# Two of thirteen norm factors: an integer guess and Newton steps on VectorE in the place of ScalarE's square root

## The chip, the cores and the metric

The kernel runs on one core of a Trainium2 chip. The metric is the device time of one execution in microseconds (us), the median of the runs shown; lower is better. The engines are TensorE (PE for its matmuls, PEld for its weight loads), VectorE (DVE), ScalarE (ACT), GpSimd (POOL) and SyncE (SP, which issues the DMAs). Each engine works through its own instructions in order; semaphores order them between engines.

## What is computed

A network of two layers on 1024 tokens of width 1024, in float32. Layer 0 mixes by sliding-window attention, layer 1 by a gated recurrence; each is followed by an MLP with a squared ReLU. Every block begins with a norm over the token's 1024 numbers:

```python
def rmsnorm(x, gain):
    y = x * lax.rsqrt(jnp.mean(jnp.square(x), axis=-1, keepdims=True) + NORM_EPS)
    return y * gain

for layer in range(2):
    h = rmsnorm(x, mix_norm[layer])
    y = attention(h, ...) if layer == 0 else recurrence(h, ...)
    x = x + y
    x = x + square(relu(rmsnorm(x, mlp_norm[layer]) @ w_up)) @ w_down
return rmsnorm(x, final_norm)
```

The factor of a token is one number, `rsqrt(mean(x*x) + eps)`. In attention the norm is taken before the projection to queries, keys and values, and the factor is applied to the projection's result, since it is the same for a whole token.

## The kernel before

The tokens are handled in two halves of 512 (`hf` 0 and 1). A matrix product in float32 is made of three fast products of parts (`mm3`: high by high, high by low, low by high), so a 512-wide weight block costs a cast to the high part (`wh`), a subtraction for the low part (`wl`) and three matmuls for each result bank.

All work is first recorded and then put in order by a planner (`Schedule.order`): it has a modelled cost for every operation and a modelled latency from engine to engine, and gives each engine, whenever it would be free, the ready operation that was recorded earliest (with leads for weights and for emptying banks). So the order in which the engines work is fixed when the program is built, and every operation that is added, removed or costed otherwise can move others. All instructions are issued from one line (L334), so the rows of the profile tell operations apart by engine, kind and the tag of the tiles: `a` long-lived 128x512 tiles, `t` short-lived ones, `m` scores and masks, `sm` tiles of 128x4, `wr`/`wh`/`wl` weights as loaded and their high and low parts, `c` constants, `p` and `q` the banks of PSUM (four each).

What the change and the argument touch:

- `token_rstd` (line 450) makes the factors of one half's tokens: four tiny matmuls (128x1 each) give the mean squares of 4 x 128 tokens in a `q` bank, a tensor_scalar adds eps (`v`, an `sm` tile), ScalarE takes a square root of 128x4 numbers, VectorE takes the reciprocal, and three VectorE operations make one Newton step (`y*y`, times `-0.5*v`, plus 1.5, times `y`).
- It is called in six places of the code. `scaled` (line 481) is one; it is used only in attention, once for each half (lines 1215 and 1219).
- `qkv` (line 1058) projects; `projected` applies the factor when it empties a `p` bank. `rope` rotates the keys and queries, and TensorE transposes them (`q<-c,t`, `q<-c,a`).
- `attend` (line 1115) transposes the queries of a group of heads, four blocks to a `q` bank (`q<-c,a`). Each bank is then read by two ScalarE instructions (`a<-q`, high parts) and two VectorE instructions (`a<-q,a`, low parts), one for each half of its rows; the bank is free for the next use when the second of the two VectorE instructions has read it.
- `attend_block` (line 1155) makes scores (`q<-a,a` and `q<-t,a`), masks them on VectorE into `m`, takes the maximum (`sm<-m`), the exponentials on ScalarE, the reciprocal of the sum and the product (`m<-m,sm`), and transposes the result (`q<-c,m`).
- Attention of half 0 is interleaved with the projection of half 1 (line 1220), so TensorE has projection matmuls (`p<-wh,a`, `p<-wl,a`) between the attention's steps.

A function on ScalarE that is not in its current table is preceded by an ACT_TABLE_LOAD, which the compiler puts in: Sqrt, Sin (the rotation tables), Exp and Tanh each bring one when the one before was another.

Of the kernel before, what the change touches and what calls it, by code (L numbers as in the profile page):

```python
# [12 lines left out]
I32 = mybir.dt.int32  # L13
AF = mybir.ActivationFunctionType
ALU = mybir.AluOpType
# [5 lines left out]
KT = D // P  # L21
NH = 2
TH = T // NH
# [256 lines left out]
class Net:  # L280
# [166 lines left out]
            acc = sq if acc is None else acc  # L447
        return acc

    def token_rstd(self, acc, inner=1.0, outer=1.0, n=TH, keep=False, more=()):  # L450

        ps = self.psum("q")
        nb = n // P
        for j in range(nb):
            parts = [acc, *more]
            for i, z in enumerate(parts):
                self.mm(ps[:, j : j + 1], z[:, j * P : j * P + P], self.mean, i == 0, i == len(parts) - 1, P, 2)
        v, y, z = (self.t(F32, (P, BPH), "sm")[:, :nb] for _ in range(3))
        self.ts("DVE", v, ps[:, :nb], inner, EPS, ALU.mult, ALU.add, 4)
        self.act(y, v, AF.Sqrt, 4)  # L460
        self.op("DVE", self.nc.vector.reciprocal, [y], [y], 100, y, y)
        self.tt("DVE", z, y, y, ALU.mult, 4)
        self.stt(z, v, -0.5 * outer, z, ALU.mult, ALU.mult, 4)
        if keep:
            y, r = self.const((P, BPH)), y
        else:
            r = y
        self.stt(y, z, 1.5 * outer, r, ALU.add, ALU.mult, 4)
        return y

    def spread(self, y, n=TH, r=None):

        r = (r or self.psum("q"))[:, :n]
        for j in range(n // P):
            self.mm(r[:, j * P : j * P + P], y[:, j : j + 1].to_broadcast([P, P]), self.ident, True, True, P, 4)
        return r
# [4 lines left out]
    def scaled(self, which, hf):  # L481

        h = []
        for kt in range(KT):
            x, gain = self.x[kt][hf], self.gain(which, kt)
            hi, lo = self.a(F32R), self.a(F32R)
            self.act(hi, x, AF.Copy, scale=gain)
            self.stt(lo, x, gain, hi.bitcast(F32), ALU.mult, ALU.subtract)
            h.append((hi, lo))
        return h, self.token_rstd(self.sum_squares([self.x[kt][hf] for kt in range(KT)]))  # L490


    def square_relu(self, m, hf, c, psum):
# [1151 lines left out]
```

## Time and profile before

| | us |
|---|---|
| median of 3 runs (2117.57 to 2119.33) | 2118.83 |
| the profiled execution, its own time | 2122.58 |
| its span on the core | 2120.8 |
| PE busy in the span | 2093.9 |
| DVE busy | 1902.4 |
| ACT busy | 1120.4 |
| DMA moved | 407 MB, 192 GB/s on the mean |

The profiled execution lies 3.75 us above the median and has 1.78 us outside the span. A busy share is an average over stages: attention (to about 300 us) is made of many short instructions on four engines, the rest of long rows of matmuls.

### The profile page before, as it was taken

The page shows a single profiled execution, that of the slowest core. Times are in us where ns is not written, and L with a number is a line of the kernel's source. Part 1 is how long each engine was busy: PE and PEld are TensorE (multiplying, and loading weights), DVE is VectorE, ACT ScalarE, POOL GpSimd, SP SyncE. Part 2 cuts the span into 40 slices and gives each one's busy share as a digit, 9 for nine tenths or more (in the row PEclk, how much of TensorE's full clock was granted, in tenths as well). Part 3 has the DMA queues.
Part 4 walks back from the last instruction along what each step waited for, and adds up shares of the span by engine and source line. Part 5 has one row for each costly group of instructions (what it writes and reads, how often), then busy time and mean ns, then how long its engine had stood idle before and what let it go on. Part 6 is the DMA issues. An engine that isn't in the chain of part 4 may idle for free.

```text
span 2120.8 us, 35631 instructions
## 1 busy us (share of the span) xinstructions
PE 2093.9 (99%) x12220; PEld 1741.4 (82%) x12220; DVE 1902.4 (90%) x3925; ACT 1120.4 (53%) x2280; POOL 60.3 (3%) x121
## 2 busy tenths in 40 slices
PE   9999999999999999999999999999999999999998
PEld 7778778888888888888888888888788888888887
DVE  8889899999999989999888888888999999898985
ACT  5567776655565323556444444452755656432453
POOL 4020000000000000000000000000000000000000
PEclk9999999999999999999999999999999999999999
DMA  6212268867778967632222222666876767896732
GB/s 205 84 52 74 87 215 272 283 224 244 230 243 285 313 222 253 221 134 75 100 95 95 100 96 87 205 231 218 272 268 227 245 227 251 283 319 217 246 108 80
DMA packets 225845, 407.43 MB, mean 192 GB/s; under 512 B 25344, under 2 KB 30464, under 8 KB 225664
## 3 DMA queue, kind: packets, MB, share of 16 engines
q1 hardware_dynamic: 225664, 405.16, 56.8%
q8 instruction: 96, 1.57, 0.3%
q14 instruction: 85, 0.70, 0.1%
HBM read 321.17 MB, written 83.89 MB: 191 GB/s over the span
## 4 chain that ended last, share of the span: by engine, by line
PE 87%; DVE 7%; issue 2%; ACT 2%; DMA 1%; POOL 0%; POOLq 0%; SPq 0%; ACTq 0%; DVEq 0%
PE p L334 46%; PE q L334 42%; DVE t L334 3%; DVE a L334 2%; DVE m L334 1%; ACT t L334 1%; ACT a L334 1%; DVE wl L334 1%; DMA a<-in_x 0%; DMA c<-in_par 0%; DVE wh L334 0%; DMA t<-d 0%; DVE sm L334 0%; DMA d<-a 0%; POOL a L334 0%
## 5 line engine op out<-in xcount | busy, mean ns | idle before, releaser
L334 PE MATMUL p<-a,wh 128*128 128x512 f32 (+1 forms) x2880 | 817.2, 367 | 0.2 <-ACT t L334 0.2
L334 PE MATMUL q<-a,wh 128*128 128x512 f32 x2112 | 662.6, 395 | 2.2 <-ACT t L334 1.7
L334 PEld LDWEIGHTS p<-a,wh 128*128 128x128 f32 x2880 | 514.3, 188 | 93.0 <-ACT t L334 0.7
L334 PE MATMUL p<-a,wl 128*128 128x512 f32 (+1 forms) x1440 | 524.1, 364 | 1.8 <-DVE wl L334 1.7
L334 PEld LDWEIGHTS q<-a,wh 128*128 128x128 f32 x2112 | 389.0, 188 | 87.1 <-ACT t L334 3.0
L334 PE MATMUL q<-a,wl 128*128 128x512 f32 x1056 | 416.0, 394 | 1.1 <-DVE wl L334 1.1
L334 PEld LDWEIGHTS p<-a,wl 128*128 128x128 f32 x1440 | 270.9, 188 | 47.0 <-DVE wl L334 3.0
L334 DVE TENSOR_TENSOR wl<-wr,wh 128x512 fp32r<-128x512 f32 x352 | 240.3, 684 | 6.4 <-ACT wh L334 1.4
L334 DVE TENSOR_TENSOR wl<-m,wh 128x512 fp32r<-128x512 f32 x338 | 230.2, 685 | 9.8 <-ACT wh L334 0.3
L334 PEld LDWEIGHTS q<-a,wl 128*128 128x128 f32 x1056 | 198.3, 188 | 47.9 <-DVE wl L334 1.5
L334 ACT ACTIVATE t<-t 128x512 f32<-128x512 f32 x266 | 167.6, 632 | 124.3 <-DVE t L334 118.3
L334 ACT CAST wh<-wr 128x512 fp32r<-128x512 f32 x247 | 152.6, 619 | 151.7 <-PE p L334 104.6
L334 DVE TENSOR_TENSOR t<-t,t 128x512 f32<-128x512 f32 (+3 forms) x337 | 196.8, 598 | 16.7 <-DMA t<-d 10.3
L334 ACT CAST a<-t 128x512 fp32r<-128x512 f32 (+1 forms) x213 | 128.3, 611 | 148.2 <-PE q L334 83.1
L334 DVE TENSOR_TENSOR a<-t,a 128x512 fp32r<-128x512 f32 (+2 forms) x314 | 205.5, 675 | 1.1 <-ACT a L334 0.8
L334 ACT CAST wh<-m 128x512 fp32r<-128x512 f32 x231 | 143.3, 621 | 111.5 <-PE p L334 48.7
L334 ACT COPY t<-q 128x512 f32<-128x512 f32 (+2 forms) x201 | 112.4, 560 | 104.6 <-PE q L334 91.4
L334 DVE TENSOR_TENSOR m<-wr,wr 128x512 f32<-128x512 f32 (+1 forms) x188 | 120.9, 645 | 15.6 <-DMA wr<-in_down 12.9
L334 PE MATMUL p<-wh,a 128*128 128x512 f32 x384 | 127.9, 404 | 2.3 <-ACT a L334 2.3
L334 DVE TENSOR_TENSOR t<-t,p 128x256 f32<-128x256 f32 x294 | 117.4, 412 | 0.2
L334 PEld LDWEIGHTS q<-t,t 128*64 128x64 f32 (+1 forms) x2160 | 95.4, 144 | 13.9 <-issue 7.8
L334 PE MATMUL q<-t,t 128*64 128x32 f32 (+2 forms) x2160 | 105.4, 229 | 0.0
(129 smaller groups left out, 2396.3 us busy)
## 6 DMA issues: line engine op xcount, KB each, us to landing
t<-d SPq DMA_DIRECT2D x548, 256.0 KB, 4.0
d<-t SPq DMA_DIRECT2D x244, 256.0 KB, 2.7
wr<-in_down SPq DMA_DIRECT2D x224, 256.0 KB, 4.2
wr<-in_up SPq DMA_DIRECT2D x178, 256.0 KB, 3.8
wr<-in_win SPq DMA_DIRECT2D x68, 256.0 KB, 2.6
a<-d SPq DMA_DIRECT2D x60, 256.0 KB, 4.5
wr<-in_wqkv SPq DMA_DIRECT2D x48, 256.0 KB, 2.7
d<-a SPq DMA_DIRECT2D x48, 256.0 KB, 3.7
```

The lines of the kernel that those rows point to most:

```text
L334: fn(*[place(a) for a in args], **{k: place(v) for k, v in kw.items()})
```

## The change

`scaled` asks for factors without the table. For these two calls the square root on ScalarE and the reciprocal on VectorE fall away. In their place stand two integer operations (shift the bits of `v` right by one, and subtract from a constant), which give a first guess of `1/sqrt(v)`, and two Newton steps more, of three operations each; the third step is the one that was there. The other eleven executions of `token_rstd` keep the square root.

```diff
-    def token_rstd(self, acc, inner=1.0, outer=1.0, n=TH, keep=False, more=()):
+    def token_rstd(self, acc, inner=1.0, outer=1.0, n=TH, keep=False, more=(), table=True):
...
         self.ts("DVE", v, ps[:, :nb], inner, EPS, ALU.mult, ALU.add, 4)
-        self.act(y, v, AF.Sqrt, 4)
-        self.op("DVE", self.nc.vector.reciprocal, [y], [y], 100, y, y)
+        if table:
+            self.act(y, v, AF.Sqrt, 4)
+            self.op("DVE", self.nc.vector.reciprocal, [y], [y], 100, y, y)
+        else:
+            self.guess(y, v)
+            for _ in range(2):
+                self.tt("DVE", z, y, y, ALU.mult, 4)
+                self.stt(z, v, -0.5, z, ALU.mult, ALU.mult, 4)
+                self.stt(y, z, 1.5, y, ALU.add, ALU.mult, 4)
         self.tt("DVE", z, y, y, ALU.mult, 4)
...
+    def guess(self, y, v):
+
+        bits = y.bitcast(I32)
+        self.ts("DVE", bits, v.bitcast(I32), 1, None, ALU.logical_shift_right, None, 4)
+        self.ts("DVE", bits, bits, -1.0, float(0x5F3759DF), ALU.mult, ALU.add, 4)
...
-        return h, self.token_rstd(self.sum_squares([self.x[kt][hf] for kt in range(KT)]))
+        return h, self.token_rstd(self.sum_squares([self.x[kt][hf] for kt in range(KT)]), table=False)
```

ScalarE has four instructions fewer (two square roots and two of eight table loads), VectorE fourteen more. Apart from the numbers in the tiles' names, the order of the five engines differs only in some hundred rows in all, and only in attention's first half.

ScalarE where attention of half 0 begins, high parts of the queries (`a<-q`), before:

```order
L334 ACTIVATE a_1037<-q_1002 64x512
L334 ACTIVATE a_1046<-q_1011 64x512
L334 ACTIVATE a_1055<-q_1011 64x512
L334 ACT_TABLE_LOAD
L334 ACTIVATE sm_1064<-sm_1059 128x4
L334 ACTIVATE a_1075<-q_1066 64x512
L334 ACTIVATE a_1079<-q_1066 64x512
```

The same place now:

```order
L334 ACTIVATE a_1043<-q_1008 64x512
L334 ACTIVATE a_1052<-q_1017 64x512
L334 ACTIVATE a_1061<-q_1017 64x512
L334 ACTIVATE a_1080<-q_1070 64x512
L334 ACTIVATE a_1084<-q_1070 64x512
L334 CAST wh_1092<-wr_918 128x512
```

The load and the square root (`sm<-sm`) are gone from between the high parts; the next load on ScalarE is the one ahead of the first exponential, as before.

VectorE at the same place, low parts of the queries (`a<-q,a`) and the factors of half 1 (`sm`), before:

```order
L334 TENSOR_SCALAR sm_1059<-q_988 128x4
L334 SCALAR_TENSOR_TENSOR a_1005<-q_995,a_1005 64x512
L334 TENSOR_TENSOR a_997<-t_1043,t_1051 128x8x8
L334 RECIPROCAL sm_1064<-sm_1064 128x4
L334 SCALAR_TENSOR_TENSOR a_1019<-q_995,a_1019 64x512
L334 TENSOR_TENSOR sm_1082<-sm_1064 128x4
L334 SCALAR_TENSOR_TENSOR a_1028<-q_1002,a_1028 64x512
L334 SCALAR_TENSOR_TENSOR sm_1082<-sm_1059,sm_1082 128x4
L334 SCALAR_TENSOR_TENSOR a_1037<-q_1002,a_1037 64x512
L334 SCALAR_TENSOR_TENSOR sm_1064<-sm_1082,sm_1064 128x4
L334 SCALAR_TENSOR_TENSOR a_1046<-q_1011,a_1046 64x512
L334 SCALAR_TENSOR_TENSOR a_1055<-q_1011,a_1055 64x512
```

The same place now:

```order
L334 TENSOR_SCALAR sm_1065<-q_994 128x4
L334 SCALAR_TENSOR_TENSOR a_1011<-q_1001,a_1011 64x512
L334 TENSOR_TENSOR a_1003<-t_1049,t_1057 128x8x8
L334 TENSOR_SCALAR sm_1077<-sm_1065 128x4
L334 SCALAR_TENSOR_TENSOR a_1025<-q_1001,a_1025 64x512
L334 TENSOR_SCALAR sm_1077<-sm_1077 128x4
L334 SCALAR_TENSOR_TENSOR a_1034<-q_1008,a_1034 64x512
L334 TENSOR_TENSOR sm_1095<-sm_1077 128x4
L334 SCALAR_TENSOR_TENSOR a_1043<-q_1008,a_1043 64x512
L334 SCALAR_TENSOR_TENSOR sm_1095<-sm_1065,sm_1095 128x4
L334 SCALAR_TENSOR_TENSOR a_1052<-q_1017,a_1052 64x512
L334 SCALAR_TENSOR_TENSOR sm_1077<-sm_1095,sm_1077 128x4
```

The reciprocal, which waits for ScalarE, is gone; a small operation on `sm` now follows each of the eight low parts (after the first one a rotation stands between), and three more come after that.

TensorE some 10 us later, where the first transposed probabilities (`q<-c,m`) come between projection matmuls, before:

```order
L334 MATMUL p_1035<-wh_965,a_665 128x512
L334 MATMUL q_1195<-c_83,m_316 128x128 x4
L334 MATMUL p_1049<-wh_965,a_512 128x512
L334 MATMUL p_1049<-wl_969,a_512 128x512
L334 MATMUL p_1049<-wh_965,a_665 128x512
L334 MATMUL p_1062<-wh_965,a_512 128x512
```

The same place now:

```order
L334 MATMUL p_1041<-wh_971,a_678 128x512
L334 MATMUL p_1055<-wh_971,a_514 128x512
L334 MATMUL p_1055<-wl_975,a_514 128x512
L334 MATMUL p_1055<-wh_971,a_678 128x512
L334 MATMUL q_1211<-c_83,m_316 128x128 x4
L334 MATMUL p_1068<-wh_971,a_514 128x512
```

The transposes stand three projection matmuls later than before.

## Rows read from the trace of the kernel before

**Rows 1.** The page: busy time of each engine, share of the span, instructions.

```profile
PE 2093.9 (99%) x12220; PEld 1741.4 (82%) x12220; DVE 1902.4 (90%) x3925; ACT 1120.4 (53%) x2280; POOL 60.3 (3%) x121
```

**Rows 2.** Windows: stretch, length, busy PE, PEld, DVE, ACT, POOL, granted clock, DMA share, GB/s.

```profile
84.00:86.50 2.50, 0.94 (x6) 0.49 (x5) 1.15 (x4) 2.43 (x5) 0.00 (x0) 1.00 0.00 0
86.50:91.00 4.50, 4.41 (x15) 3.39 (x15) 4.28 (x8) 0.96 (x2) 0.00 (x0) 0.62 0.00 0
91.00:107.00 16.00, 16.00 (x92) 13.55 (x91) 14.41 (x31) 11.74 (x42) 0.68 (x3) 1.00 0.30 100
...
240.00:300.00 60.00, 56.77 (x342) 43.63 (x340) 52.68 (x104) 48.31 (x140) 0.48 (x2) 0.97 0.42 145
300.00:2121.00 1821.00, 1804.82 (x10657) 1512.38 (x10656) 1641.99 (x3304) 921.33 (x1704) 13.15 (x23) 1.00 0.61 205
```

**Rows 3.** Groups of ScalarE's instructions: count, busy us, mean ns, idle before.

```profile
L334 ACT ACT_TABLE_LOAD x8 | 10.3, 1283 | 0.8 <-PEq L1613 0.7
...
L334 ACT ACTIVATE sm<-sm 128x4 f32<-128x4 f32 (+1 forms) x13 | 2.6, 204 | 31.0 <-DVE sm L334 30.9
```

**Rows 4.** Timeline at half 1's factors: start us, us, instruction, count [idle before, releaser].

```profile
82.21 0.15 DVE L334 TENSOR_SCALAR sm<-q 128x4 f32<-128x4 f32 x1
82.38 0.69 DVE L334 SCALAR_TENSOR_TENSOR a<-q,a 64x512 fp32r<-64x512 f32 x1
83.08 0.23 DVE L334 TENSOR_TENSOR a<-t,t 128x64 f32<-128x64 f32 x1
...
83.72 1.28 ACT L334 ACT_TABLE_LOAD   x1
84.12 0.39 PE L334 MATMUL p<-wl,a 128*128 128x512 f32 x1
84.35 0.40 PE L334 MATMUL p<-wh,a 128*128 128x512 f32 x1
85.02 0.21 ACT L334 ACTIVATE sm<-sm 128x4 f32<-128x4 f32 x1
85.25 0.18 DVE L334 RECIPROCAL sm<-sm 128x4 f32<-128x4 f32 x1 [1.95 <-ACT sm L334]
85.46 0.69 DVE L334 SCALAR_TENSOR_TENSOR a<-q,a 64x512 fp32r<-64x512 f32 x1
...
86.30 0.36 PE L334 MATMUL q<-a,a 128*128 128x256 f32 x1 [1.55 <-DVE a L334]
86.38 0.68 DVE L334 SCALAR_TENSOR_TENSOR a<-q,a 64x512 fp32r<-64x512 f32 x1
...
88.21 2.85 DVE L334 SCALAR_TENSOR_TENSOR a<-q,a 64x512 fp32r<-64x512 f32 x4
```

**Rows 5.** Timeline after it, 92 to 116 us.

```profile
92.22 0.40 PE L334 MATMUL q<-t,a 128*128 128x256 f32 x2
93.25 0.68 DVE L334 TENSOR_REDUCE sm<-m 128x4 f32<-128x516 f32 x1
97.26 0.47 PEld L334 LDWEIGHTS q<-c,m 128*128 128x128 f32 x4 [0.17 <-ACT m L334]
106.81 0.43 DVE L334 CAST wh<-wr 128x512 fp32r<-128x512 f32 x1 [0.47 <-PE p L334]
115.56 0.69 DVE L334 TENSOR_TENSOR t<-q,c 128x512 f32<-128x512 f32 x1 [0.85 <-PE q L334]
```

**Rows 6.** Timeline at half 0's factors and after it, 24 to 41 us.

```profile
24.51 0.16 DVE L334 TENSOR_SCALAR sm<-q 128x4 f32<-128x4 f32 x1 [1.82 <-PE q L334]
24.59 0.17 DVE L334 TENSOR_SCALAR c<-c 128x8 f32<-128x8 f32 x1
24.71 0.20 ACT L334 ACTIVATE sm<-sm 128x4 f32<-128x4 f32 x1 [2.54 <-DVE sm L334]
30.21 0.48 DVE L334 SCALAR_TENSOR_TENSOR t<-p,sm,a 128x256 f32<-128x256 f32 x1 [0.53 <-PE p L334]
40.55 0.44 PE L334 MATMUL q<-c,t 128*128 128x128 f32 x2 [0.38 <-DVE t L334]
```

## The prediction

> **What bounds the kernel now.** I read the page's busy times first, then the windows stage by stage, then the timeline at the two places that the change touches. TensorE is busy for 2093.9 of 2120.8 us [rows 1], so a saving counts only where TensorE stands still or runs at half clock. From 300 us to the end it is busy for 1804.8 of 1821 us at full clock [rows 2], and the program there is unchanged row for row: whatever attention's first half saves or loses is carried to the end as a shift. So two questions are left: does TensorE wait for the factors, directly or through a queue, at half 0's (24 us) and at half 1's (82 us)?
>
> At half 1's it does, through two queues. ScalarE loads a table at 83.72, takes the root at 85.02, and only then goes on with the high parts. VectorE's queue has the reciprocal of that root ahead of the second low part, and stands still for 1.95 us, until 85.25. The second low part (85.46 to 86.15) is the last reader of a PSUM bank; TensorE's first score matmul, which takes that bank over, starts at 86.30 after 1.55 us of idleness [rows 4]. Neither needs the factors: these are applied some 30 us later. Then the granted clock is 0.62 over the 4.5 us to 91 [rows 2], a mix of the two levels 2.4 and 1.2 GHz, which costs 4.5 x 0.38 = 1.7 us. Together some 3.3 us are lost here, the price of one root of 128x4 numbers.
>
> **Half 1's factors, step by step.** Removed: a load of 1.28 us, a root of 0.21 and VectorE's wait of 1.95. In place of one reciprocal and three small operations there are eleven, seven more. What a small operation costs between two low parts I take from the spacing of the low parts: 88.21 plus 2.85 us for four in a row is one every 0.71, and 85.46 to 86.38 with one small operation between is 0.92 [rows 4]. So 0.21 us each, and this also covers operations that depend on the one before, since a low part lies between them.
>
> VectorE now: the rotation that starts at 83.08 ends its turn at about 83.3; with the first guess the second low part starts at 83.5 (before 85.46), and the others follow every 0.92: 84.4, 85.3, 86.3, 87.2, 88.1 and 89.0. Before, the last started at 88.21 + 3 x 0.71 = 90.34. The four banks become free earlier by 1.96, 1.95, 1.74 and 1.32 us: the extra operations eat a third of the gain by the fourth. ScalarE is ahead all the while, since without load and root its last high part is done at about 85.
>
> TensorE now: its matmuls of 512 columns start 0.23 us apart (84.12 and 84.35 [rows 4]), those of 256 columns about half that. Walking through its rows from 84.35 with these times, and 0.12 us from the end of a low part to the waiting matmul (86.15 to 86.27 or so), it waits 0.07 us at the second score matmul, 0.57 for the low part that starts at 86.3, then 0.11, 0.26 and 0.37 us: 1.4 us in five pieces, in the place of 1.55 in one. If the clock stays at its upper level, the score matmuls that ended at 92.44 before (the row at 92.22, two of them [rows 5]) end at 90.26, with one projection matmul more done: 2.4 us gained. If it falls as before, the half-clock matmuls cover the waits and the gain is the shift of the banks, 1.3 to 1.95 us. I take 2.4, since the pieces are short and the longest is a third of the 1.55 us after which the clock fell.
>
> **What is late next.** VectorE. From 91 to 107 us it is busy for 14.4 of 16 us [rows 2], and four of the small operations come after the last low part. With these its first maximum (93.25 before [rows 5]) comes earlier by 1.32 - 4 x 0.21 = 0.5 us if there was no idle moment before it to take them, by 1.3 if there were enough; I take 0.9, the middle. The first transposed probabilities wait for that chain: their weight load stood still for 0.17 us at 97.26 [rows 5]. They now stand three projection matmuls later, 0.7 us. TensorE would reach them at 97.36 - 2.4 + 0.7 = 95.7 and find them ready at about 97.3 - 0.9 = 96.4: 0.7 us are given back, and 1.7 are left. After that VectorE can catch up, because it waited for TensorE itself, 0.47 us at 106.81 and 0.85 at 115.56 [rows 5]. I leave 1.7. Between 124 and 300 us the waits depend on what TensorE hands over, and move with it.
>
> **Half 0's factors.** Before, ScalarE waited 2.54 us at the head of its queue for `v` [rows 6], but TensorE had no wait there. The ScalarE time that comes free, a load and a root, hides behind matmuls and counts zero. VectorE gets eight operations for the reciprocal, and two constants' operations move to about 42 us: five more before 30.21, at 0.08 (the spacing at 24.51 and 24.59 [rows 6]) to 0.21 us: 0.4 to 1.05 us. It had 0.53 us of idleness just before 30.21, so it begins to empty the banks 0 to 0.5 us late. TensorE needs the first bank again only three blocks later, about 2 us after 30.2, and the bank takes 0.8 us to empty: nothing. Next in line is the last key transpose, which waited 0.38 us at 40.55 [rows 6]; VectorE's lateness would add to it, but the transpose now stands nine projection matmuls later, behind more VectorE work. Bounds: 0.4 us gained to 0.5 lost; I take zero.
>
> The Trainium skill speaks against the change here: "VectorE: DVE Perf Modes", section "The DRAIN you can't avoid", says that the next operation does not start until the pipe is empty, and its rules for kernel authors say to minimise the count of operations. By that the five cost their whole 0.16 us each or more, and the upper end above would be the value; the time would be 0.5 us more than I forecast. The trace does not agree with the first half of it: an operation of 0.16 us is followed after 0.08 by the next one.
>
> **The sum.** 0 + 2.4 - 0.7 = 1.7 us less. The profiled execution's 2122.58 us (span 2120.8 and 1.78 around it) becomes 2120.9; the median of the runs lies 3.75 below, so 2118.83 becomes 2117.1. With both ends of each term the forecast's own range is a gain of 0.9 to 2.8 us, 2116.0 to 2118.0. About 0.2%, 4.2 us, is what a measurement of this kernel can tell from no change, so even the best of this is "the same".
>
> **The rivals.**
> - *The gain is swallowed.* VectorE is short of time from 84 to 107 us and the seven more operations stay in its queue; if TensorE's other waits on it there (the 0.17 us at 97.26 shows how close they run) take the rest, TensorE is where it was by 107 us: 2118.3 to 2119.3. For it: 14.4 of 16 us busy. Against it: VectorE itself waited for TensorE at 106.81 and 115.56 [rows 5].
> - *Both clock dips go.* From 240 to 300 us the granted clock is 0.97 [rows 2], a second loss of 60 x 0.03 = 1.8 us, which a shifted or shortened wait may spare, as it may bring a new one. With 2.4 to 3 us at 84 us that is 4.2 to 4.8: 2114.0 to 2114.6, at the bound of "faster". For it: nothing in the rows of that place changes, so only the moment; that is also what speaks against it.
> - *VectorE becomes the bound and the kernel is slower.* Mechanism: a dependent small operation costs more than 0.21 us, for the integer ones no row shows a price. Half 1's seven more take back VectorE's 1.95 us and the 0.7 of cover when each costs (1.95 + 0.7) / 7 = 0.38 us, nearly twice the row's. From there every 0.1 us more delays TensorE by 0.7, and a wait of 1.5 us or more brings a clock dip of 1.7 with it as at 86.30. At 0.5 us TensorE is 0.8 late and the dip is there as before: 2119.7; with a dip more at 40 us, where five operations at 0.5 exceed the 0.53 of idleness by 2 us, 2121.4; at 0.7 us (1.4 more at half 1's, and the wait at 40 us itself) 2123.
> - *The change does not do what it says.* If the compiler still loaded a table at these places, only the reciprocal's wait would shorten. The built order shows six loads for eight [rows 3] and no root among the high parts, so I give it nothing.
>
> **How the numbers follow.** Forecast 0.60 (2116.0 to 2118.0), swallowed 0.18, both dips gone 0.12, slower 0.10. A median's own scatter is about 1 us (2117.57 to 2119.33). The range that holds 8 in 10 takes the forecast, the swallowed case and the near part of the two others: 2114.4 to 2119.8. Faster by over 0.2% (below 2114.6): half of the dips' case, 0.06. Slower by over 0.2% (above 2123.1): the far part of the last, 0.04. Same: 0.90.
>
> **What would show it.** In the changed trace VectorE's wait for `ACT sm` at 83 us is gone and its low parts start 0.92 us apart from 83.5; TensorE's idle before the score matmuls is in several pieces of under 0.6 us; the granted clock from 84 to 91 us is near 1.00; the first maximum starts about 0.9 us earlier, by 107 us TensorE is about 1.7 us ahead, and everything from 300 us on is shifted by as much. The forecast is wrong if the small operations space the low parts by clearly more than 0.92, if the clock falls there all the same, or if the lead at 107 us is not found again at 300.

## The result

| | before | after |
|---|---|---|
| median, us | 2118.77 (20 runs, 2117.28 to 2120.57) | 2122.94 (20 runs, 2119.88 to 2124.92) |
| own time of the profiled execution, us | 2122.58 | 2121.62 |
| its span, us | 2120.8 | 2119.8 |

The changed kernel is slower: ratio 1.0018, 95% interval 1.0012 to 1.0024, some 4 us. The forecast was 1.7 us less, and 2122.94 lies above its range. One run of an experiment below, of the kernel with one row moved back, took 4717.82 us and is left out of its median. The two profiled executions alone would say the opposite, so the first thing to settle is why they mislead. The windows of the first 20 us (columns as in [rows 2]), before and then after:

```profile
0.00:20.00 20.00, 16.51 (x64) 13.74 (x65) 15.21 (x36) 12.92 (x23) 6.04 (x21) 0.91 0.83 278
```

```profile
0.00:20.00 20.00, 17.64 (x74) 14.38 (x75) 15.66 (x38) 13.42 (x24) 6.45 (x22) 1.00 0.84 278
```

The profiled execution of before began its 100th matmul 2.28 us later than that of after, on rows that are the same: its first matmul of 512 columns starts at 7.27 us (after: 5.92), and from 8.8 to 12.2 us it ran at half clock. That start alone turns the sign of this comparison. It is not the only slow start. In five of the other profiles the matmuls of 512 columns start 0.43 us apart up to 9 to 10.5 us and 0.23 later, though their windows read 1.00 as well. One such row, of the second profile of after (0.63 us; later it is 0.39 to 0.40):

```profile
7.23 0.63 PE L334 MATMUL p<-wh,a 128*128 128x512 f32 x1
```

These five begin their 100th matmul 0.7 to 1.2 us before that of before, the six others 1.4 to 2.6. So I compare medians between kernels, and within the traces places, counted by matmul. The table has the start of the k-th matmul in a trace less the start of the k-th in the trace of before, in us (worked out from the traces; in brackets when that matmul starts before). These five matmuls are the same row in all the kernels.

| k-th matmul | 100 (27.5) | 300 (73.9) | 400 (95.5) | 600 (133.4) | 1400 (269.0) |
|---|---|---|---|---|---|
| after | -2.28 | +1.92 | -0.38 | -0.53 | -0.65 |
| a second profile of after | -1.19 | +2.60 | +0.31 | +0.13 | +0.14 |
| guess for half 0 only | -1.22 | +2.87 | +2.13 | +2.50 | +2.53 |
| guess for half 1 only | -2.43 | -1.26 | -3.56 | -3.69 | -3.74 |
| half 1 only, rotations paired | -0.79 | -1.36 | -3.64 | -3.81 | -3.87 |
| before, rotations paired | -0.69 | -0.67 | -1.39 | -1.11 | -1.08 |
| the same again | -2.38 | -2.38 | -2.30 | -2.20 | -2.15 |
| after, one row moved back | -2.33 | -1.32 | -3.62 | -3.79 | -3.84 |
| after, rotations paired | -2.62 | -1.88 | -4.16 | -4.35 | -4.40 |
| new operations, old order | -1.37 | -0.13 | -1.50 | -1.23 | -1.28 |
| old operations, new order | -0.71 | +3.02 | +0.81 | +0.69 | +0.60 |

Read along the first row: 4.2 us are lost between the 100th and the 300th matmul, 2.3 are won back by the 400th, and little changes up to the 1400th. (From the third row on they belong to the experiments below.) The forecast knew the second step and had the first at zero. Net that is 1.6 us, 1.3 in the second profile, and not the 4.2 and 3.6 by which the medians differ. The trace of before holds a half clock at 87 us that not every execution has (0.7 to 0.8 us, below); the one to two us that remain have no place in these rows. The forecast also carried its sum to the end as a mere shift. Past the 1400th matmul all kernels have the same rows, but by the last matmul the profiles have moved against that of before by 2.6 us down to 2.2 up. The page and the windows of after show the clock; they answer [rows 1] and [rows 2], with one stretch more ahead:

```profile
PE 2093.1 (99%) x12220; PEld 1739.5 (82%) x12220; DVE 1905.3 (90%) x3939; ACT 1117.7 (53%) x2276; POOL 60.9 (3%) x121
```

```profile
42.00:46.00 4.00, 2.91 (x8) 2.40 (x9) 3.87 (x10) 1.04 (x4) 3.67 (x5) 0.57 0.22 69
84.00:86.50 2.50, 2.50 (x15) 2.07 (x14) 2.36 (x9) 2.43 (x5) 0.00 (x0) 1.00 0.00 0
86.50:91.00 4.50, 4.26 (x23) 2.99 (x23) 4.19 (x11) 2.30 (x5) 0.00 (x0) 1.00 0.00 0
91.00:107.00 16.00, 15.84 (x88) 13.13 (x87) 15.00 (x36) 11.02 (x41) 1.69 (x3) 1.00 0.30 100
240.00:300.00 60.00, 56.80 (x342) 43.56 (x340) 52.08 (x103) 48.13 (x140) 0.45 (x2) 0.97 0.43 142
```

From 84 to 91 us TensorE now works (2.50 of 2.50 us and 15 matmuls, where [rows 2] had 0.94 and 6) and the clock stays at 1.00. In its place the clock falls at 42 to 46 us, where TensorE is busy for only 2.91 of 4 us.

**What happens at 43 us.** The timeline of after, rows of TensorE (without its projection matmuls), VectorE and ScalarE in order of time:

```profile
38.54 2.25 ACT L334 CAST a<-q 64x128 fp32r<-64x128 f32 x8
39.14 0.59 DVE L334 TENSOR_TENSOR t<-q,a 64x128 fp32r<-64x128 f32 x2
39.65 0.28 DVE L334 TENSOR_TENSOR t<-t,t 128x32 f32<-128x32 f32 x1
40.81 1.14 ACT L334 CAST wh<-wr 128x512 fp32r<-128x512 f32 x2
41.46 0.78 DVE L334 TENSOR_TENSOR wl<-wr,wh 128x512 fp32r<-128x512 f32 x1 [1.53 <-ACT wh L334]
42.27 0.59 DVE L334 TENSOR_TENSOR t<-q,a 64x128 fp32r<-64x128 f32 x2
42.79 0.25 DVE L334 TENSOR_TENSOR t<-t,t 128x32 f32<-128x32 f32 x1
43.09 0.69 PE L334 MATMUL q<-c,t 128*128 128x128 f32 x2 [2.63 <-DVE t L334]
```

The last key block is rotated by two VectorE operations (`t<-t,t` of 128x32, the first and the second half of a head's numbers), and TensorE transposes it when both are done. The first stands at 39.65, the second at 42.79, and each takes 0.25 to 0.28 us. Between them VectorE has a weight's low part (41.46). That one needs ScalarE's high part (40.81), which stands behind eight casts of key parts (38.54 to 40.79). So VectorE stands still for 1.53 us with rows behind it that do not need this high part, and TensorE waits 2.63 us for a 0.25 us operation. The same place before ([rows 6] has its transpose, at 40.55 with 0.38 us of waiting):

```profile
38.83 0.19 DVE L334 TENSOR_TENSOR t<-t,t 128x32 f32<-128x32 f32 x1
...
39.42 2.25 ACT L334 CAST a<-q 64x128 fp32r<-64x128 f32 x8
39.70 0.59 DVE L334 TENSOR_TENSOR t<-q,a 64x128 fp32r<-64x128 f32 x2
40.30 0.19 DVE L334 TENSOR_TENSOR t<-t,t 128x32 f32<-128x32 f32 x1
...
41.70 0.62 ACT L334 CAST wh<-wr 128x512 fp32r<-128x512 f32 x1
```

The same eight casts, but the second half of the rotation (40.30) ran while they were under way; the low part that waits for the cast at 41.70 came behind it. VectorE's order as the planner wrote it, before and after, shows the swap (`t_497` and `t_499` are the last key block, twice each; `wl_638` and `wl_636` the same weight):

```
before                                          after
TENSOR_TENSOR t_497<-t_589,t_591 128x4x8        TENSOR_TENSOR t_499<-t_609,t_614 128x4x8
...                                             TENSOR_TENSOR wl_636<-wr_417,wh_627 128x512
TENSOR_TENSOR t_497<-t_589,t_591 128x4x8        TENSOR_TENSOR t_259<-q_554,a_281 64x128
...                                             TENSOR_TENSOR t_239<-q_590,a_264 64x128
TENSOR_TENSOR wl_638<-wr_417,wh_619 128x512     TENSOR_TENSOR t_499<-t_609,t_614 128x4x8
```

None of the rows in that piece is new. The planner takes the oldest row that is ready by its model; with more operations ahead on VectorE the modelled times shift, and the low part must have counted as ready earlier. Its modelled times were not read.

**The place at 82 to 92 us** went as forecast. VectorE in after (the operations of 128x4 are the factors, those of 64x512 the low parts), then TensorE's only wait of over 0.2 us:

```profile
84.99 0.23 DVE L334 TENSOR_TENSOR a<-t,t 128x64 f32<-128x64 f32 x1
85.14 0.16 DVE L334 TENSOR_SCALAR sm<-sm 128x4 int32<-128x4 int32 x1
85.33 0.69 DVE L334 SCALAR_TENSOR_TENSOR a<-q,a 64x512 fp32r<-64x512 f32 x1
86.05 0.17 DVE L334 TENSOR_SCALAR sm<-sm 128x4 int32<-128x4 int32 x1
86.25 0.68 DVE L334 SCALAR_TENSOR_TENSOR a<-q,a 64x512 fp32r<-64x512 f32 x1
...
88.82 0.39 PE L334 MATMUL q<-a,a 128*128 128x256 f32 x1 [0.24 <-DVE a L334]
```

VectorE's 1.95 us [rows 4] are gone, the low parts stand 0.92 us apart, and an integer operation costs what the others do.

### The profile page after: what moved, and what is told of

Its sections match the earlier page's. It is cut to its first block, busy times and chain, and to the rows that moved or that the text cites. A ratio compares the mean times of both kernels' runs of the same rounds, so it can differ in the third digit from the quotient of the medians.

```text
span 2119.8 us, 35639 instructions
## 1 busy us (share of the span) xinstructions
PE 2093.1 (99%) x12220; PEld 1739.5 (82%) x12220; DVE 1905.3 (90%) x3939; ACT 1117.7 (53%) x2276; POOL 60.9 (3%) x121
## 3 DMA queue, kind: packets, MB, share of 16 engines
q8 instruction: 96, 1.57, 0.3%
## 4 chain that ended last, share of the span: by engine, by line
PE 86%; DVE 8%; issue 2%; ACT 2%; DMA 1%; SPq 0%; POOL 0%; POOLq 0%; ACTq 0%; DVEq 0%
PE p L334 45%; PE q L334 41%; DVE t L334 3%; DVE a L334 2%; DVE m L334 1%; ACT t L334 1%; DVE wl L334 1%; ACT a L334 1%; DMA a<-in_x 1%; DMA t<-d 0%; DVE wh L334 0%; DMA wr<-in_up 0%; ACT wh L334 0%; SPq L334 0%; DVE sm L334 0%
## 5 line engine op out<-in xcount | busy, mean ns | idle before, releaser
L334 PEld LDWEIGHTS q<-t,t 128*64 128x64 f32 (+1 forms) x2160 | 95.5, 144 | 14.0 <-issue 7.8
```

The costliest lines, as they stand in the source:

```text
L334: fn(*[place(a) for a in args], **{k: place(v) for k, v in kw.items()})
```

## The experiments

The theory from these two traces: the loss is the order, not the arithmetic; it belongs to half 0's call, which changes VectorE's rows ahead of 40 us; and moving one row back removes it. The rivals: the fourteen operations cost more than they seem to; or the loss is a clock that falls by chance.

**The changed kernel again**, for a second trace and for a time on the chip of the next three kernels.

> The changed kernel once more, for a second profile beside its first. The order theory (the planner moved rows at 34 to 48 us; there TensorE waits 2.6 us at the last key transpose and then runs at half clock for about 3.5 us) expects the same wait and the same dip again and a time of 2122 to 2124 us. The scatter theory (the difference between the two kernels is made of clock dips that come and go from execution to execution) expects the dips elsewhere than in the first profile, or fewer, and times that overlap with those of before.

2122.92 us (11 runs) against 2119.36 for before: ratio 1.0016 (1.0008 to 1.0025). TensorE's wait, and the window around it:

```profile
43.45 0.67 PE L334 MATMUL q<-c,t 128*128 128x128 f32 x2 [2.67 <-DVE t L334]
```

```profile
34.00:50.00 16.00, 13.30 (x54) 10.20 (x53) 13.27 (x36) 9.56 (x28) 13.42 (x20) 0.89 0.29 104
```

The wait and the half clock behind it are there again.

**One row moved back.** In the changed kernel the second half of the last key rotation is put directly ahead of the low part that waits for ScalarE. All arithmetic stays.

```diff
-        for op in self.order():
+        for op in moved(self.order()):
...
+def moved(done):
+    on_dve = lambda *names: [op for op in done if op.engine == "DVE" and set(names) <= {b.name for b in op.bufs}]
+    low, rope = on_dve("wl149")[0], on_dve("t121", "t122", "t123")[1]
+    done.remove(rope)
+    done.insert(done.index(low), rope)
+    return done
```

> The changed kernel with one VectorE row moved: the second half of the last key block's rotation stands ahead of the weight's low part (the one that waits for a high part on ScalarE) instead of three rows behind it. All else is as in the changed kernel, the fourteen more operations too. The order theory expects the wait of 2.6 us before the last key transpose to be gone or under 0.4 us, no dip at 42 to 46 us, and 4.2 us less than the changed kernel: 2118.7 us. The rival, that the fourteen operations themselves make VectorE late, expects no more than 0.5 us less than the changed kernel: 2122.4 us.

2118.75 us (11 runs), 4.2 less than the changed kernel on the same chip; against before 0.9997 (0.9988 to 1.0006). VectorE, TensorE's transpose, and the window:

```profile
39.77 0.39 DVE L334 TENSOR_TENSOR t<-t,t 128x32 f32<-128x32 f32 x2
41.59 0.78 DVE L334 TENSOR_TENSOR wl<-wr,wh 128x512 fp32r<-128x512 f32 x1 [1.43 <-ACT wh L334]
```

```profile
40.40 0.38 PE L334 MATMUL q<-c,t 128*128 128x128 f32 x2
```

```profile
34.00:50.00 16.00, 15.40 (x69) 12.18 (x69) 13.43 (x37) 9.30 (x27) 13.71 (x20) 1.00 0.31 108
```

VectorE stands still for as long as it did (1.43 us for 1.53), but nobody waits behind it: the transpose runs at 40.40 without a wait and the clock stays up. By the medians one row in its place is worth the whole loss. In the traces 3.2 of the 4.2 us between the 100th and the 300th matmul are gone; the 1.0 that is left holds a wait of 0.60 us at the third key transpose (36.40) and one of 0.53 at 54.78.

**One half's factors at a time.** `scaled` passes `table=hf == 1` (guess for half 0 only) or `table=hf == 0` (for half 1 only) in the place of `table=False`.

> Half 0's factors by the guess, half 1's by the square root as before. By the order listing the rows up to 60 us are those of the changed kernel and the later ones those of before. The order theory expects the wait at the last key transpose with its dip, and the wait before the first score matmul as in before: before plus 4.2 us, 2123.0 us. The rival of the operations' own cost expects half of the whole difference: 2120.9 us.

> Half 1's factors by the guess, half 0's by the square root as before. By the order listing the rows up to 60 us are those of before and the later ones those of the changed kernel. My prediction's term for this place (1.7 us gained, 2.7 between the two profiles) expects 2116.1 to 2117.1 us and no wait of over 0.6 us before the score matmuls. The rival of the operations' own cost expects it slower than before: 2120.9 us. If the wait at 85 us costs a clock dip only in some executions, the gain is nearer to 1.0: 2117.8 us.

Half 0 only: 2123.21 us, ratio 1.0019 (1.0010 to 1.0027). Half 1 only: 2118.01 us, 0.9994 (0.9986 to 1.0003). TensorE's waits of over a microsecond in the first and its windows, then those of the second:

```profile
43.75 0.44 PE L334 MATMUL q<-c,t 128*128 128x128 f32 x2 [2.65 <-DVE t L334]
89.18 0.36 PE L334 MATMUL q<-a,a 128*128 128x256 f32 x1 [1.51 <-DVE a L334]
```

```profile
34.00:50.00 16.00, 13.16 (x53) 9.99 (x53) 13.23 (x39) 9.87 (x28) 13.14 (x20) 0.89 0.32 112
80.00:92.00 12.00, 10.10 (x57) 7.86 (x56) 9.76 (x31) 7.85 (x13) 0.00 (x0) 1.00 0.06 23
```

```profile
36.39 0.44 PE L334 MATMUL q<-c,t 128*128 128x128 f32 x2 [1.24 <-DVE t L334]
```

```profile
34.00:50.00 16.00, 14.38 (x64) 11.11 (x63) 13.36 (x37) 9.40 (x27) 13.72 (x20) 1.00 0.31 106
80.00:92.00 12.00, 11.56 (x60) 8.85 (x59) 11.49 (x35) 8.36 (x18) 0.00 (x0) 1.00 0.07 22
```

The loss is half 0's (3.9 us over before), a small gain is half 1's (1.35, with an interval that holds zero), less than was expected. The table shows 1.17 us lost between the 100th and the 300th matmul ahead of the 2.30 gained by the 400th, and at the third key transpose TensorE waits 1.24 us, where before has nothing of that size. That is not of the edit: up to 80 us TensorE, VectorE and ScalarE have the rows of before, in the same order. But this execution comes there earlier. ScalarE waits for a DMA of `x` ahead of the casts, the rotation and this transpose, and goes on only 1.28 us earlier than in the trace of before, while TensorE is 2.43 us ahead at the 100th matmul. ScalarE in half 1 only, then in before:

```profile
33.07 1.40 ACT L334 ACTIVATE a<-a,c 128x512 fp32r<-128x512 f32 x2 [1.99 <-DMA a<-in_x]
```

```profile
34.35 1.40 ACT L334 ACTIVATE a<-a,c 128x512 fp32r<-128x512 f32 x2 [1.42 <-DMA a<-in_x]
```

So a part of what a trace loses in this stretch can be an early start that is used up. What does bear on the small gain is this: in the first of the two kernels the 1.51 us wait at 89.18, which the old half 1 still has, is followed by a window at clock 1.00: the half clock that [rows 2] showed behind this wait is not in every execution. Where it is absent the old half 1 gets from the 300th to the 400th matmul 0.74 us sooner than in the trace of before, so that much less is there to be gained.

**The arithmetic and the order taken apart.** First the new operations in the old order: the planner is told of a root and a reciprocal as before, and the eight VectorE operations are issued in one row at the reciprocal's place. Then the reverse: root and reciprocal, but the planner is told of the new operations, so that the rows stand as in the changed kernel.

```diff
 # new operations, old order
+            self.s.add({"ACT": (lambda: None, 94 + 4 * 0.834)}, [y], [v])
+            self.op("DVE", self.guess_and_steps, [y, z], [y, v], 100, y, v, z)
 # old operations, new order
+            nothing = lambda *a: None
+            self.op("DVE", self.nc.scalar.activation, [y], [v], 68 + 4 * 0.52, y, v, AF.Sqrt)
+            self.op("DVE", self.nc.vector.reciprocal, [y], [y], 68 + 4 * 0.52, y, y)
+            for _ in range(2):
+                self.op("DVE", nothing, [z], [y], 70 + 4 * 1.04)
...
```

> The guess and the Newton steps, but the planner is told of the square root and the reciprocal, so that all other rows stand as in the kernel before; the eight new operations stand in a row where each reciprocal stood, and the roots and their table loads are gone. The order theory (the loss is made by the rows that the planner moved) expects no wait of over 1.5 us before the last key transpose, and at half 1's factors eight dependent operations at 0.21 us, 1.7 us, in place of the wait of 1.95: 0.2 to 0.7 us less than before. The rival (the fourteen operations cost it on VectorE) expects 2 to 4 us more than before, as in the changed kernel.

> The square root and the reciprocal as before, but the planner is told of the guess and all nine steps, so that all other rows stand as in the changed kernel. The order theory expects the wait of about 2.6 us before the last key transpose although VectorE has none of the fourteen operations, and the wait of about 1.5 us before the first score matmuls: before plus 3.9 us. The rival of the operations' cost expects the time of before within 1 us.

The old operations in the new order: 2122.50 us against 2119.22, ratio 1.0014 (1.0005 to 1.0023), with none of the fourteen operations in it. VectorE's low part and TensorE's wait:

```profile
42.29 0.74 DVE L334 TENSOR_TENSOR wl<-wr,wh 128x512 fp32r<-128x512 f32 x1 [1.57 <-ACT wh L334]
```

```profile
43.89 0.44 PE L334 MATMUL q<-c,t 128*128 128x128 f32 x2 [2.64 <-DVE t L334]
```

This settles it against the rival: the order alone makes the loss. By the table it loses 3.7 us between the 100th and the 300th matmul, where the three traces with the new half 0 in this order lose 3.8 to 4.2.

The same run says something of half 1 that was not expected of it. The load, the root and the reciprocal are all there, but in the changed kernel's order the reciprocal stands behind the second low part instead of ahead of it:

```profile
88.27 0.18 DVE L334 RECIPROCAL sm<-sm 128x4 f32<-128x4 f32 x1 [1.24 <-ACT sm L334]
```

```profile
89.30 0.36 PE L334 MATMUL q<-a,a 128*128 128x256 f32 x1 [0.92 <-DVE a L334]
```

TensorE waits 0.92 us in the place of 1.55 (about 1.5 was expected), no half clock follows, and from the 300th to the 400th matmul the trace wins 2.2 us against that of before, where the changed kernel wins 2.3. By these traces nearly all of the gain at half 1, too, is the place of a row, and the arithmetic is worth about 0.1 us of it.

The new operations in the old order gave 2120.61 us, 1.0006 (0.9997 to 1.0015): neither the small gain that was expected nor the 2 to 4 us of the rival, and not told from before. TensorE waits 0.48 and 0.52 us at the third and the last key transpose. The trace shows what eight dependent operations cost with nothing between them, and what is left of TensorE's wait behind them:

```profile
83.09 0.16 DVE L478 TENSOR_SCALAR sm<-sm 128x4 int32<-128x4 int32 x1
83.28 0.17 DVE L479 TENSOR_SCALAR sm<-sm 128x4 int32<-128x4 int32 x1
83.49 0.16 DVE L481 TENSOR_TENSOR sm<-sm 128x4 f32<-128x4 f32 x1
83.69 0.16 DVE L482 SCALAR_TENSOR_TENSOR sm<-sm,sm 128x4 f32<-128x4 f32 x1
```

```profile
85.50 0.35 PE L334 MATMUL q<-a,a 128*128 128x256 f32 x1 [0.89 <-ACT wh L334]
```

One every 0.20 us, 1.57 for all eight, against the 1.95 us wait that they replace. From the 300th to the 400th matmul this wins 1.4 us against the trace of before, 0.6 against the guess for half 0 only, which has no half clock there. In this order, in one row, the guess is worth little.

**Every key rotation kept together.** A rule in the place of one moved row: the second half of each key block's rotation is issued right behind its first. It was put into the changed kernel and into the kernel before.

```diff
-        for op in self.order():
+        for op in paired(self.order(), self):
...
+        if heads == NG:
+            PAIRS.append(self.s.ops[-2:])
...
+def paired(done, schedule):
+    for first, second in [p for p in PAIRS if p[0] in schedule.ops]:
+        done.remove(second)
+        done.insert(done.index(first) + 1, second)
+    return done
```

> The changed kernel, with the second half of each key block's rotation directly behind its first half on VectorE (seven such rows moved up, nothing else). The order theory expects the waits before the third and the last key transpose (0.5 and 2.6 us in the changed kernel) to be gone, with the dip behind the second: 4.5 us less than the changed kernel, some 0.7 us less than before. The rival of the operations' cost expects less than 1 us off the changed kernel.

> The kernel before, with the second half of each key block's rotation directly behind its first half. If the order of these rows is a weakness that the kernel before already had (in the run with half 1 alone changed, which has its rows there, TensorE waited 1.2 and 0.4 us before the third and the last key transpose), it gains 1.0 to 1.6 us over before; if only the changed kernel's rows are hit, nothing.

The changed kernel comes to 2119.12 us, 1.0000 (0.9992 to 1.0009), the one before to 2118.04, 0.9996 (0.9987 to 1.0005), both against 2119.22. The first removes the loss once more, by another edit, but lies 0.1 us under before and not the 0.7 that was expected; its longest wait from 20 to 92 us is 0.75, at 54.23. That the second is faster than before isn't shown by its interval.

**Half 1's factors with the rotations kept together**, without half 0's: the best of the parts. Beside it, on the same chip, the paired rotations with the square roots.

> Guess and steps for half 1 only, and each key block's second rotation half directly behind its first on VectorE. If the gain at half 1's place is independent of the rotations' order (theory), the two gains add: only_half1 lay 1.35 us under the kernel before and pairs_before 1.18, so 2.5 us under it, near 2116.7 where the kernel before gives 2119.2; no TensorE wait over 0.8 us and no half clock between 20 and 50 us, and pieces of under 0.3 us at 85 to 92. If both gains are the same microsecond (rival: the first shift is absorbed at the later place, where VectorE is short of time), it is no faster than either alone, 2117.9 to 2118.1.

> The paired rotations with the square roots, again, on the same chip as half1_pairs, so that the difference of the two is half 1's factors by themselves. Theory: 1.2 to 2.4 us slower than half1_pairs (the 1.55 us wait at 85.6 is back, with a half clock behind it in some executions), about 1.2 us under the kernel before. Rival: within 0.4 us of half1_pairs.

2116.86 us (2116.09 to 2119.03, 11 runs) and 2119.67 (2117.05 to 2120.23, 11 runs), against 2119.41 for before: 0.9991 (0.9982 to 1.0000) and 0.9996 (0.9987 to 1.0005). The first is the fastest kernel seen here, 2.55 us under before, where 2.5 was expected, with 1.0000 the upper end of its interval. The sum behind that 2.5 isn't confirmed: the paired rotations by themselves lay 1.18 us under before on one chip and lie 0.26 above it by the medians on this one, where about 1.2 under was expected. The difference of the two kernels, 2.8 us by the medians and 2.0 by the means, lies above the 1.35 of the guess for half 1 alone; by the table the site itself gives 2.28 against the trace of before in this kernel as in the others, and 1.6 against the first trace of the paired rotations, which has no half clock there. So half 1's change, operations and order together, is worth about 1.4 to 2.8 us, and these runs do not fix it closer. The first one's windows and its only wait of over 0.2 us between 80 and 92 us:

```profile
34.00:50.00 16.00, 16.00 (x75) 12.99 (x74) 14.32 (x41) 10.03 (x28) 13.07 (x19) 1.00 0.37 117
...
80.00:92.00 12.00, 11.56 (x60) 8.85 (x59) 11.49 (x35) 8.35 (x18) 0.00 (x0) 1.00 0.08 22
```

```profile
85.56 0.39 PE L334 MATMUL q<-a,a 128*128 128x256 f32 x1 [0.28 <-DVE a L334]
```

The paired rotations with the square roots were profiled twice, one kernel on two chips. Wait and window of the first, then of the second:

```profile
85.63 0.36 PE L334 MATMUL q<-a,a 128*128 128x256 f32 x1 [1.55 <-DVE a L334]
```

```profile
80.00:92.00 12.00, 10.06 (x51) 7.58 (x50) 9.63 (x28) 8.57 (x16) 0.00 (x0) 1.00 0.00 0
```

```profile
83.92 0.36 PE L334 MATMUL q<-a,a 128*128 128x256 f32 x1 [1.55 <-DVE a L334]
```

```profile
80.00:92.00 12.00, 10.36 (x47) 7.95 (x46) 9.40 (x20) 7.91 (x14) 0.00 (x0) 0.86 0.08 21
```

The same wait of 1.55 us of the same kernel is followed by half clock in the second and not in the first. By the clock alone, 0.86 for 12 us, the second would pay 12 x 0.14 = 1.7 us more; by their two rows of the table it takes 0.8 us more from the 300th to the 400th matmul (+0.08 for -0.72).

## Why the prediction was wrong

- **Where TensorE would feel the change, half 1: right on the place and the wait.** VectorE's wait for the root, at the head of its queue, was the cause of the 1.55 us; the low parts came 0.92 apart as worked out; TensorE's pieces were 0.24 and 0.16 us of idleness by the profile, some 1.1 us in all, by an estimate, when counted from start to start as the prediction counted its 1.4; the clock stayed up. The 2.4 us gained at the site measured 2.3 against that trace of before. But "the price of one root" it was not: the old operations in the new order, with load and root, win 2.2 of it. By these traces it was mostly the price of the order there, with a reciprocal that stood one low part too early. The Trainium skill, "ScalarE: Activation LUTs", section "What ACT_TABLE_LOAD costs", counts a drain of about 1.38 us with each load; this trace shows none behind the load at 83.72, the root starts 1.30 us later [rows 4].
- **The 0.7 us given back at the first transposed probabilities: not there.** In the six traces with the new half 1 in its own order the lead at the 600th matmul is 0.1 to 0.2 us more than at the 400th.
- **The price of the half clock at 86.5 to 91 us: too high.** The prediction put it at 1.7 us from the granted clock. Between executions with it and without it the site differs by 0.7 to 0.8 us. At half clock TensorE takes longer over matmuls in whose time it would have waited for low parts: without it there is a wait more, 0.31 us at 91.92 in the guess for half 0 only. The forecast's 2.4 did not rest on that price, since it came from walking through the rows; but it was set against a dip that only some executions have, and was 1.6 against one without. The rival with both dips priced the second one, at about 295 us, at 1.8; with it the stretch from the 1400th to the 1600th matmul takes 38.5 to 38.8 us, without it 37.2 to 37.3, and both profiles of the changed kernel still have it.
- **The 3.75 us between the profiled execution and the median** were subtracted as one constant. The start of that execution is 0.7 to 2.6 us behind the others at the 100th matmul, and the dip at 87 us took 0.7 to 0.8; the rest isn't explained.
- **Half 0's factors at zero, with bounds from 0.4 gained to 0.5 lost: this is the step that failed.** It measured 3.9 us lost (half 0 only), 3.8 to 4.2 in the traces between the 100th and the 300th matmul. Of the 4.2, 2.63 and 0.49 us are waiting, for the 0.38 that was there, and the half clock from 42 to 46 is 4 x 0.43 = 1.7 by the clock: 4.4 together. The prediction priced the extra VectorE operations, found cover for them, and was right that they cost no more than 0.21 us each. But it took the order of the rows around the last key transpose as a mere shift: it noted that the transpose "now stands nine projection matmuls later, behind more VectorE work" (eight in the traces), and did not ask of each of these VectorE rows what it waits for itself. One of them, the low part, waits for ScalarE, 1.53 us in the changed kernel. The rows to find it were in reach: the order of after has the low part ahead of the rotation, and ScalarE's order has its high part behind eight casts, which [rows 6]'s stretch shows to last 2.25 us.
- **The slower rival had the right place and the wrong mechanism.** It put a wait and a dip at 40 us, and 2121.4 us, on small operations that cost 0.5 us. They cost 0.20, and the wait came without them (the old operations in the new order). The Trainium skill's advice to minimise the number of operations ("VectorE: DVE Perf Modes", section "Rules for kernel authors") doesn't explain the loss: the same number of operations with one row moved back shows no loss against before (0.9997).
- **0.90 for "the same" by 0.2%** stands at the edge of what was measured (+0.18% by the ratio, +0.20% by the medians); the direction was wrong. That 0.2% "is what a measurement of this kernel can tell from no change" was too coarse: 20 runs of each kernel gave the ratio to 0.06% on either side.

What stays open: what half 1's factors are worth in a median to better than a microsecond; where the one to two us stand by which the medians differ more than the traces up to the 1400th matmul; and why a wait of one length is followed by half clock in some executions only. That the half clock behind the 2.6 us wait belongs to that wait is seen in four profiles of four; it was not tried apart from it.

## What to carry to other kernels

Where a planner fixes the order, price a change by the order that it leaves, not by the operations it adds: on every in-order queue ahead of a place where the bound engine waits, look for a row that itself waits for a third engine and that now stands ahead of the row the bound engine needs. Both places of this case are of that kind, the low part at 41 us and the reciprocal at 85. Check a profiled execution against its median before taking sizes from it, and ask of every clock dip in it whether a second execution has it too. A step made of two operations that one consumer needs together is safer issued together.

## What the runs showed of the hardware

- Dependent VectorE operations on 128x4 tiles start 0.20 us apart in a row, integer and float alike (0.16 to 0.17 us each); between two low parts one adds 0.21.
- A TensorE wait of 2.63 to 2.67 us was followed by half clock in each of the four profiles that have it. One of 1.51 to 1.55 us was followed by it in two profiles (before, and the second of the paired rotations), and not in two others (half 0 only, and the first of the paired rotations). The wait of 1.70 us at about 295 us is in all profiles; the window from 240 to 300 us reads 0.97 or 0.98 in eight of them and 1.00 in four.
- Half clock hides waits: 4.5 us at a granted clock of 0.62 cost 0.7 to 0.8 us where matmuls waited for VectorE anyway, against 1.7 by the clock alone. The one at about 295 us cost 1.2 to 1.6.
- At the start the window's granted clock does not tell all: one of twelve profiles reads 0.91 for the first 20 us and the others 1.00, but in five of these the matmuls of 512 columns start 0.43 us apart, as at half clock, up to 9 to 10.5 us.
